# Division by the sums behind the product with the values, in a hybrid layer of pooling and sliding-window attention

## Chip, cores and metric

The kernel runs on one core of a Trainium2 chip. Its time is the device time of one launch in microseconds (us); smaller is better. A core has TensorE (PE: products of matrices, and the loads of their weights, PEld), VectorE (DVE), ScalarE (ACT), GpSimd (POOL) and SyncE (SP, which issues most transfers). They run side by side, each through its own list of instructions in order, and wait for one another by semaphores. SBUF is the working memory of 128 partitions, PSUM holds TensorE's results in eight banks.

## The reference

One layer, 1024 tokens, width 1024, all in float32. What is computed, cut to what matters:

```python
h = rmsnorm(x, norm_pre)
pool_u, pool_gate, q, k, v, attn_gate = split(h @ w_in)          # widths 512, 512, 512, 128, 128, 512
# pooling: trailing means over 2, 4, 8 and 16 tokens (one window for each 128 channels), minus the token
pooled = means(pool_u) - pool_u
pool_out = (pooled @ w_grp per group) * scale * silu(pool_gate)
# attention: 8 heads of 64, 2 heads of keys and values, blocks of 128 queries against 256 keys
scores = q @ k.T * 64 ** -0.5 - slope * distance                 # window of 128, causal
probs  = softmax(concat([scores, sink], -1))[..., :-1]           # one sink logit for each head
attn_out = (probs @ v) * silu(attn_gate)
y = concat([pool_out, attn_out]) @ w_out
x = x + rmsnorm(y, norm_post)
```

So a row of probabilities is exp(score - m) over the sum of these and exp(sink - m), with m the largest of the row and the sink.

## The kernel before

Every product in float32 is made of three float16 products: an operand is scaled by a power of two and split into a high and a low half (`split`: ScalarE writes the high half, VectorE the low one). The power of two comes from a bound: ScalarE sums absolute values (`bound_w`), TensorE spreads the 128 sums over the partitions (`spread`), VectorE reduces them (`widest`) and makes the scale (`pow2_of`, together `scale_w`).

Ahead of the loop x is normed and transposed into `hT`, and the weights of K, V and Q are prepared; `v_tile` makes V in eight pieces. Then a written-out order runs over slots s = 5 to 33. A slot is one projection of 128 channels by 512 tokens (`proj`, 24 matmuls): the rest of K and Q for the second half of the tokens (5 to 9), the pool's gates `pg` (10 to 17), the pool's inputs `u` (18 to 25) and the attention's gates `ag` (26 to 33). `land_slot` takes each result out of PSUM. All instructions stand in the order in which the code names them; nothing reorders them later.

Block n of attention has slots 5 + 2n and 6 + 2n. In the even one of a pair `score_mm` makes the scores (four banks), `score_land` scales them on VectorE, adds the bias and reduces the maximum, and ScalarE makes eight exponentials with their sums. `soft` (odd slot) adds the sink's exponential, takes the reciprocals (8 for each query) and GpSimd multiplies the 1024 values. `turn` (next even slot) splits them into `ph`, which a transposing transfer turns into `full`; `mask` (odd) cuts it on GpSimd by two selections into the block's own keys and the previous ones; `pv_mm` (two slots after that) makes the product with V, which ScalarE takes into `cat`, ahead of the gate.

For a weight of slot s0, `bound_w` stands in slot s0 - 3, `spread_w` at the end of s0 - 2, `scale_w` at the start of s0 - 1. Weights come by `load_next` in the order of `loads_in_order` through four buffers, each load once a buffer is given up. The pool's windows (`pool_windows`, VectorE) follow one slot behind their input, `pool_mm` one more. After the last slot TensorE runs 16 products of the output projection (`out_mm`) back to back.

PSUM: three banks for projections and V (`ps_acc`), four (`ps_b`, taken by `bank`) for scores, transposes, spread bounds and the pool, one for the product with the values. The names that the rows use: `st` the scores, `negm` the negated maximum, `whl` a split weight, `wraw` and `woraw` raw weights, `amall` a reduced bound, `ws` its scale, `wom` the output weight's bound, `acc` a projection, `tp` a transpose, `pv` a piece of V.

Of the kernel before, what the change touches and what calls it, by code (L numbers as in the profile page):

```python
# [35 lines left out]
def trunk(ctx: ExitStack, tc, x, w_in, pool_w, pool_scale, attn_sinks, w_out, norm_pre, norm_post, out):  # L36
# [21 lines left out]
    def work(name):  # L58
        return t4.tile([P, S], F32, tag="t4", name=name)
# [201 lines left out]
    def v_tile(tt):  # L261
        w = whl[V]
        pv = ps_acc.tile([P, 512], F32, tag="acc", name="pv")[:, :P]
# [15 lines left out]
    nsinks = const.tile([P, 8], F32, name="nsinks")  # L279
    pscale = const.tile([P, 4], F32, name="pscale")  # L280
    pw = const.tile([P, 4, P], F32, name="pw")
    post = const.tile([P, D], F32, name="post")
# [16 lines left out]
    def constants():  # L299
        nc.gpsimd.tensor_scalar(nsinks, sinks, -1.0, 0.0, op0=ALU.mult, op1=ALU.add)  # L300
# [29 lines left out]
    att_sc, att_s, att_p, att_f = {}, {}, {}, {}  # L330
# [18 lines left out]

    def score_land(n):  # L350
        st = work("st").rearrange("p (h s) -> p h s", s=P)
        for pr in range(2):
            for kv, sc in enumerate(att_sc.pop((n, pr))):
                hs = slice(4 * kv + 2 * pr, 4 * kv + 2 * pr + 2)
                if n:
                    nc.vector.copy_predicated(sc[:, :, 0, :], own_key.bitcast(U16), sc[:, :, 1, :])  # L356
                nc.vector.scalar_tensor_tensor(  # L357
                    st[:, hs, :], sc[:, :, 0 if n else 1, :], qu[:, 2 * pr : 2 * pr + 1],
# [13 lines left out]
        nc.scalar.activation(es, es, AF.Exp)  # L372
        att_s[n] = (st, sums, es)

    def soft(n):
        st, sums, es = att_s[n]
        nc.vector.tensor_tensor(sums, sums, es, op=ALU.add)
        r = small.tile([P, 8], F32, tag="r", name="r")
        nc.vector.reciprocal(r, sums)
        nc.gpsimd.tensor_tensor(st, st, r.unsqueeze(2).broadcast_to([P, 8, P]), op=ALU.mult)  # L380


    def turn(n):
        st = att_s.pop(n)[0]
        ph = att.tile([P, 2, 8, P], F16, tag="ph", name="ph")
        split(st, 4096.0, ph[:, 0], ph[:, 1])
# [3 lines left out]
        )  # L390
        att_f[n] = full

# [16 lines left out]

    def pv_mm(n):  # L410
# [4 lines left out]
        for tt, t in parts:  # L415
# [60 lines left out]
    def land_slot(ch, half, acc):  # L476
# [6 lines left out]
        elif kind == "pg":  # L483
            nc.scalar.activation(cat[:, c, hs], acc, AF.Silu, scale=wu[ch])
# [28 lines left out]
    def open_late():  # L513
        att.release()
        lp = ctx.enter_context(tc.tile_pool(name="late", bufs=1, reuse_waits="tile"))
        late["wo"] = lp.tile([P, 2, KT, D], F16, name="wo")

# [47 lines left out]
    def out_last(n):  # L565
        o, xr = work(f"o{n}"), residue.pop(n)
        for nh in range(2):
            hs = half_of(nh)
            acc = out_mm(n, nh)
            nc.vector.tensor_tensor(o[:, hs], acc, post[:, hs], op=ALU.mult)  # L570
# [9 lines left out]
    def out_store(n, accs):  # L580
# [4 lines left out]
        for nh, acc in enumerate(accs):  # L585
            hs = half_of(nh)
            nc.vector.scalar_tensor_tensor(  # L587
                o[:, hs], acc, f, post[:, hs], op0=ALU.mult, op1=ALU.mult
# [5 lines left out]
    with tc.manual_schedule(engines={ENG.PE, ENG.Activation, ENG.DVE, ENG.Pool, ENG.SP}):  # L594
# [87 lines left out]
        def loads_in_order():  # L682
            for i in range(3):
                yield "w", PGS[i]
            yield "b", 0
            yield "w", PGS[3]
            for k in range(1, 6):
                yield "b", k
            yield "w", US[0]
            yield "b", 6  # L690
            yield "w", US[1]
            yield "b", 7
            for ch in US[2:] + AGS:
                yield "w", ch
# [15 lines left out]
        wo_bound = split_done = 0  # L710
        last = len(slots)
        for s in range(5, last):
# [4 lines left out]
            for key in list(spreads):  # L717
                if key[0] == "c":
                    scale_cat(key[1])
                elif key[0] == "wo":  # L720
                    pow2_of(widest(spreads.pop(key)), wop, wos, 14)
                else:
                    scale_w(key)
# [105 lines left out]
```

## Time and profile before

| | us |
|---|---|
| median of 3 runs | 388.57 |
| lowest and highest | 387.72, 389.57 |
| the profiled execution | 391.86 |
| its span, first to last instruction | 390.1 |
| TensorE busy in the span | 334.8 (86%) |
| VectorE busy | 205.1 (53%) |
| ScalarE busy | 178.9 (46%) |
| GpSimd busy | 75.6 (19%) |
| TensorE's granted clock, share of 2.4 GHz | 0.949 |

Busy time is a sum over stages that differ, so it doesn't tell what bounds; a stage's own waits do. Matmuls overlap and their ends are modelled, so a busy TensorE isn't one at its peak. The times of the table's first two lines come from runs without the profiler.

### The profile page before, as it was taken

The numbers are of one execution on the slowest core, as the hardware profiler recorded it, in microseconds if no ns is written. First come the engines' busy times: TensorE is split into PE (matmuls) and PEld (weight loads), VectorE is DVE, ScalarE is ACT, GpSimd is POOL, SyncE is SP. The second block draws the span as 40 slices with busy tenths as digits, with TensorE's granted clock in tenths as the row PEclk, the third lists the DMA queues.
The fourth block names the chain that finished last, engine by engine and source line by source line (L and its number), as shares of the span: only waits on it lengthen the run. The fifth ranks groups of instructions, "written<-read, shape, count | busy, mean of one in ns | idle before, by whom it ended". The sixth has DMA issues, their size and how long they took to land.

```text
span 390.1 us, 4820 instructions
## 1 busy us (share of the span) xinstructions
PE 334.8 (86%) x1783; PEld 161.2 (41%) x1783; DVE 205.1 (53%) x435; ACT 178.9 (46%) x374; POOL 75.6 (19%) x74
## 2 busy tenths in 40 slices
PE   3487799999796969908995999997999999999993
PEld 1355557444342424403441344442444444444441
DVE  2776563326665736438388854677467144441122
ACT  5656552054639484884834322355546323321110
POOL 1101023010141414160504140000000033333330
PEclk9999699999896999966999699999999999999998
DMA  7963303002243745535251240045810022225111
GB/s 275 247 177 83 109 2 109 0 2 54 60 103 108 161 103 115 86 78 126 50 108 41 55 109 0 4 154 146 244 48 0 0 89 86 84 95 172 70 55 54
DMA packets 52089, 35.71 MB, mean 92 GB/s; under 512 B 35041, under 2 KB 45793, under 8 KB 52066
## 3 DMA queue, kind: packets, MB, share of 16 engines
q1 hardware_dynamic: 52064, 35.40, 34.1%
q8 instruction: 14, 0.23, 0.2%
q14 instruction: 9, 0.07, 0.1%
q10 hardware_dynamic: 2, 0.00, 0.0%
HBM read 27.01 MB, written 4.19 MB: 80 GB/s over the span
## 4 chain that ended last, share of the span: by engine, by line
PE 37%; DVE 27%; ACT 17%; issue 11%; POOL 4%; DMA 2%; SPq 0%; DVEq 0%; POOLq 0%; ACTq 0%
PE acc L259 20%; PE y L259 11%; ACT st L368 4%; ACT whl L93 4%; DVE st L357 3%; POOL o L590 3%; DVE win L452 2%; DVE sc L356 2%; PE pv L259 2%; DVE whl L94 2%; DVE negm L363 2%; DVE negm L362 2%; DVE ph L94 2%; ACT whl L90 2%; DVE wo L94 2%
## 5 line engine op out<-in xcount | busy, mean ns | idle before, releaser
L259 PE MATMUL acc<-hT,whl 128*128 128x512 f16 x816 | 190.4, 391 | 8.0 <-ACT whl L93 5.2
L259 PEld LDWEIGHTS <-whl 128*128 128x128 f16 x816 | 79.6, 100 | 114.1 <-issue 16.7
L259 PE MATMUL y<-wo,chl 128*128 128x512 f16 x384 | 83.5, 379 | 0.0
L259 PEld LDWEIGHTS <-chl 128*128 128x128 f16 x384 | 37.6, 98 | 44.5
L368 ACT ACTIVATE st<-st,negm 128x128 f32<-128x128 f32 x64 | 24.8, 388 | 42.2 <-DVE negm L363 42.2
L94 DVE SCALAR_TENSOR_TENSOR whl<-wraw,ws,whl 128x1024 f16<-128x1024 f32 x18 | 23.1, 1294 | 28.9 <-ACT whl L93 27.6
L559 ACT ACTIVATE junk<-y 128x512 bf16<-128x512 f32 x16 | 9.6, 597 | 57.1 <-PE y L259 57.1
L93 ACT ACTIVATE whl<-wraw,ws 128x1024 f16<-128x1024 f32 x18 | 20.4, 1144 | 29.7 <-DVE ws L76 29.7
L561 DVE SCALAR_TENSOR_TENSOR eps_of<-yss,eps_of 128x1 f32<-128x1 f32 x16 | 4.6, 288 | 48.3 <-ACT junk L559 48.1
L400 POOL TENSOR_SCALAR_AFFINE_SELECT own<-full 128x2048 f16<-128x2048 f16 x7 | 14.0, 2006 | 66.5 <-DMA full<-ph 52.1
L380 POOL TENSOR_TENSOR st<-st,r 128x1024 f32<-128x1024 f32 x8 | 15.2, 1896 | 56.8 <-ACT whl L90 19.5
L582 POOL TENSOR_TENSOR yf<-eps_of,mhalf 128x1 f32<-128x1 f32 x7 | 3.9, 551 | 108.1 <-DVE eps_of L561 108.1
L342 PE MATMUL sc<-kT,qT 64*128 64x256 f16 (+1 forms) x192 | 15.4, 297 | 9.3 <-DVE amall L86 8.8
L243 PE MATMUL tp<-ident,h 128*128 128x128 f32 x64 | 12.9, 368 | 11.8 <-DVE h L234 10.8
L590 POOL TENSOR_TENSOR o<-o,xr 128x512 f32<-128x512 f32 x14 | 17.4, 1268 | 17.7 <-DVE o L587 13.9
L90 ACT ACTIVATE whl<-wraw 128x1024 bf16<-128x1024 f32 x18 | 18.8, 1047 | 0.0
L94 DVE SCALAR_TENSOR_TENSOR qT<-acc,qT 128x512 f16<-128x512 f32 x8 | 5.5, 691 | 22.8 <-ACT qT L93 22.8
L243 PEld LDWEIGHTS tp<-ident,h 128*128 128x128 f32 x64 | 10.6, 193 | 15.3 <-DVE h L234 6.8
L259 PE MATMUL pv<-whl,hT 128*128 128x128 f16 x192 | 12.6, 230 | 4.2 <-DVE vst L94 4.2
L342 PEld LDWEIGHTS <-qT 64*128 64x128 f16 x192 | 9.7, 103 | 15.1 <-issue 12.3
L357 DVE SCALAR_TENSOR_TENSOR st<-sc,qu,bias 128x256 f32<-128x256 f32 x32 | 15.2, 483 | 1.1
L94 DVE SCALAR_TENSOR_TENSOR chl<-cat,cs,chl 128x1024 f16<-128x1024 f32 x8 | 10.3, 1284 | 10.2 <-ACT chl L93 10.2
(106 smaller groups left out, 371.2 us busy)
## 6 DMA issues: line engine op xcount, KB each, us to landing
wraw<-in_w_in_dram SPq DMA_DIRECT2D x10, 512.0 KB, 4.4
x<-in_x_dram SPq DMA_DIRECT2D x8, 512.0 KB, 5.6
wraw<-in_w_in_dram SPq DMA_DIRECT2D x16, 256.0 KB, 4.0
woraw<-in_w_out_dram SPq DMA_DIRECT2D x8, 512.0 KB, 4.2
woraw<-in_w_out_dram SPq DMA_DIRECT2D x16, 256.0 KB, 4.8
xr<-in_x_dram SPq DMA_DIRECT2D x8, 512.0 KB, 3.6
out_dram<-o SPq DMA_DIRECT2D x16, 256.0 KB, 2.0
post<-in_norm_post_dram SPq DMA_DIRECT2D x1, 512.0 KB, 4.7
```

Source lines behind the costliest of these rows:

```text
L90: nc.scalar.activation(junk, src, AF.Abs, accum_out=m)
L93: nc.scalar.activation(hi, src, AF.Copy, scale=s)
L94: eng.scalar_tensor_tensor(lo, src, s, hi, op0=ALU.mult, op1=ALU.subtract)
L243: nc.tensor.transpose(flips[tt][b][:, block_of(i)], h[:, block_of(4 * b + i)], ident)
L259: nc.tensor.matmul(acc, a, b, start=i == 0, stop=i == len(pairs) - 1)
L342: nc.tensor.matmul(banks[kv][:, ci, k0:, :], qT[rows, a, 2 * pr + ci, block_of(n)], kT[rows, b, (n - 1 + k0) * P : (n + 1) * P], start=i = ...
L357: nc.vector.scalar_tensor_tensor(st[:, hs, :], sc[:, :, 0 if n else 1, :], qu[:, 2 * pr : 2 * pr + 1], (bias if n else bias0)[:, hs, :], o ...
L368: nc.scalar.activation(st[:, h, :], st[:, h, :], AF.Exp, bias=negm[:, h : h + 1], accum_out=sums[:, h : h + 1],)
L380: nc.gpsimd.tensor_tensor(st, st, r.unsqueeze(2).broadcast_to([P, 8, P]), op=ALU.mult)
L400: nc.gpsimd.affine_select(o, f, pattern=[[0, 16], [1, P]], compare_op=ALU.is_ge, fill=0.0, base=0, channel_multiplier=-1,)
L559: nc.scalar.activation(junk, acc, AF.Square, accum_out=q)
L590: nc.gpsimd.tensor_tensor(o[:, hs], o[:, hs], xr[:, hs], op=ALU.add)
```

## The change

The values of a block are no longer divided by their sums ahead of the split. `turn` stands in the odd slot of the block, directly behind the exponentials, `mask` in the next even one, `pv_mm` in the next odd one. VectorE takes the reciprocals with each sum repeated 64 times (512 elements for each query); in the next even slot `divide` turns them by four transposes on TensorE, ScalarE puts them into `cat` with V's scale, and VectorE multiplies the product with V into that. The sink is a 129th score column, copied in by VectorE, so the maximum and the sums hold it. `Silu` of the pool's gates is taken out of `land_slot` and done in slots 20 to 23, in place, on 1024 elements. Spread bounds, and the transposed reciprocals, have a bank of their own (`ps_sp`); `ps_acc` has two banks instead of three, and V's pieces take theirs from the four of `ps_b`. A weight is spread and scaled at the start of s0 - 2. The weights of the gates and inputs are loaded ahead of the output weight's first pass, whose bounds move from slots 8 to 18 to slots 19 to 22; the split of the output weight starts once its bound is there. `post` lives in a later pool and is loaded when that opens, at slot 22.

The diff, cut to its core:

```diff
-    ps_acc = ctx.enter_context(tc.tile_pool(name="ps_acc", bufs=3, space=PSUM))
+    ps_acc = ctx.enter_context(tc.tile_pool(name="ps_acc", bufs=2, space=PSUM))
+    ps_sp = ctx.enter_context(tc.tile_pool(name="ps_sp", bufs=1, space=PSUM))
...
     def spread(m):
-        t = bank("spread", P)
+        t = ps_sp.tile([P, 512], F32, tag="sp", name="spread")[:, :P]
...
     def v_tile(tt):
-        pv = ps_acc.tile([P, 512], F32, tag="acc", name="pv")[:, :P]
+        pv = bank("pv", P)
...
     def score_land(n):
-        st = work("st").rearrange("p (h s) -> p h s", s=P)
+        st = t4.tile([P, S + 8], F32, tag="t4", name="st").rearrange("p (h s) -> p h s", h=8)
+        nc.vector.tensor_copy(st[:, :, P], sinks)
...
         nc.vector.tensor_reduce(negm, st, axis=AX.X, op=ALU.max, negate=True)
-        nc.vector.tensor_tensor(negm, negm, nsinks, op=ALU.min)
-        es = small.tile([P, 8], F32, tag="es", name="es")
-        nc.vector.tensor_tensor(es, sinks, negm, op=ALU.add)
...
-        nc.scalar.activation(es, es, AF.Exp)
-        att_s[n] = (st, sums, es)
-
-    def soft(n):
-        st, sums, es = att_s[n]
-        nc.vector.tensor_tensor(sums, sums, es, op=ALU.add)
-        r = small.tile([P, 8], F32, tag="r", name="r")
-        nc.vector.reciprocal(r, sums)
-        nc.gpsimd.tensor_tensor(st, st, r.unsqueeze(2).broadcast_to([P, 8, P]), op=ALU.mult)
+        att_s[n] = (st, sums)
...
     def turn(n):
-        st = att_s.pop(n)[0]
+        st, sums = att_s.pop(n)
...
+        r = t2.tile([P, 512], F32, tag="t2", name="r")
+        nc.vector.reciprocal(
+            r.rearrange("p (c kv d) -> p c kv d", c=4, kv=2),
+            sums.rearrange("p (kv c) -> p c kv", kv=2).unsqueeze(3).broadcast_to([P, 4, 2, HD]),
+        )
...
+    def divide(n):
+        r = att_r.pop(n)
+        rb = ps_sp.tile([P, 512], F32, tag="sp", name="rb")
+        for c in range(4):
+            nc.tensor.transpose(rb[:, block_of(c)], r[:, block_of(c)], ident)
+        nc.scalar.activation(
+            cat[:, 4:8, block_of(n)], rb.rearrange("p (c t) -> p c t", t=P), AF.Copy, scale=vo
+        )
...
-        nc.scalar.activation(
-            cat[:, 4:8, block_of(n)], pv.rearrange("p (c t) -> p c t", t=P), AF.Copy, scale=vo
-        )
+        dst = cat[:, 4:8, block_of(n)]
+        nc.vector.tensor_tensor(dst, pv.rearrange("p (c t) -> p c t", t=P), dst, op=ALU.mult)
...
         elif kind == "pg":
-            nc.scalar.activation(cat[:, c, hs], acc, AF.Silu, scale=wu[ch])
+            nc.scalar.activation(cat[:, c, hs], acc, AF.Copy, scale=wu[ch])
...
         def loads_in_order():
-            for i in range(3):
-                yield "w", PGS[i]
-            yield "b", 0
-            yield "w", PGS[3]
-            for k in range(1, 6):
+            for ch in PGS + US:
+                yield "w", ch
+            for k in range(6):
                 yield "b", k
...
+                elif first_slot[key] == s + 2:
+                    spread_w((key,))
+                    scale_w((key,))
                     freed += 1
             if not odd:
                 if 1 <= n <= NB:
-                    turn(n - 1)
+                    mask(n - 1)
                 if n < NB:
                     score_mm(n)
             else:
+                if n < NB:
+                    turn(n)
                 if 1 <= n <= NB:
-                    mask(n - 1)
-                if 2 <= n <= NB + 1:
-                    pv_mm(n - 2)
-                if n < NB:
-                    soft(n)
+                    pv_mm(n - 1)
             acc = proj(ch, half)
...
+            if 20 <= s < 24:
+                gate = cat[:, 23 - s, :]
+                nc.scalar.activation(gate, gate, AF.Silu)
...
-            if not odd and n < NB:
-                score_land(n)
+            if not odd:
+                if n < NB:
+                    score_land(n)
+                if 1 <= n <= NB:
+                    divide(n - 1)
```

VectorE's order in one pair of slots with two weights, from the maximum of block 2. Before (`sums` and `r` are the softmax's, the three rows from `amall` make a weight's scale):

```order
L362 TENSOR_REDUCE negm<-st 128x8
L363 TENSOR_TENSOR negm<-negm,nsinks 128x8
L365 TENSOR_TENSOR es<-sinks,negm 128x8
L94 SCALAR_TENSOR_TENSOR qT<-acc,qT 128x512
L86 TENSOR_REDUCE amall<-spread 128x1
L72 TENSOR_SCALAR wp<-amall 128x1
L75 TENSOR_SCALAR wp<-wp 128x1
L76 RECIPROCAL ws<-wp 128x1
L94 SCALAR_TENSOR_TENSOR whl<-wraw,ws,whl 128x1024
L216 TENSOR_TENSOR wu<-wp,gsc 128x1
L377 TENSOR_TENSOR sums<-sums,es 128x8
L379 RECIPROCAL r<-sums 128x8
```

and after the change, from the same maximum:

```order
L362 TENSOR_REDUCE negm<-st 128x8
L95 SCALAR_TENSOR_TENSOR qT<-acc,qT 128x512
L87 TENSOR_REDUCE amall<-spread 128x1
L73 TENSOR_SCALAR wp<-amall 128x1
L76 TENSOR_SCALAR wp<-wp 128x1
L77 RECIPROCAL ws<-wp 128x1
L95 SCALAR_TENSOR_TENSOR whl<-wraw,ws,whl 128x1024
L217 TENSOR_TENSOR wu<-wp,gsc 128x1
L95 SCALAR_TENSOR_TENSOR ph<-st,ph 128x1024
L381 RECIPROCAL r<-sums 128x512
L430 TENSOR_TENSOR cat<-pvo,cat 128x4x128
L87 TENSOR_REDUCE amall<-spread 128x1
```

The two instructions on the sinks are gone; the split `ph` of the same block has come up behind the first weight, and a reciprocal of 512 elements and the product with the values stand between it and the second weight.

GpSimd's order over the same blocks (`st` scaled by `r`, then the two selections). Before:

```order
L380 TENSOR_TENSOR st_871<-st_871,r_894 128x1024
L380 TENSOR_TENSOR st_985<-st_985,r_1012 128x1024
L400 AFFINE_SELECT own_1164<-full_1065 128x2048
L404 AFFINE_SELECT full_1065<-full_1065 128x2048
L380 TENSOR_TENSOR st_1123<-st_1123,r_1176 128x1024
```

and after:

```order
L395 AFFINE_SELECT own_1082<-full_1025 128x2048
L399 AFFINE_SELECT full_1025<-full_1025 128x2048
L395 AFFINE_SELECT own_1250<-full_1188 128x2048
L399 AFFINE_SELECT full_1188<-full_1188 128x2048
L395 AFFINE_SELECT own_1383<-full_1339 128x2048
```

GpSimd's scaling has gone; the selections alone are left.

## Rows read from the trace of the kernel before

**Rows 1.** Busy time by stretch: us, then engines (instructions), PEclk, DMA share, GB/s.
```profile
0.00:74.24 74.24, 55.78 (x384) 36.31 (x385) 38.86 (x79) 36.38 (x65) 10.42 (x30) 0.95 0.47 132
74.24:89.18 14.94, 14.42 (x104) 7.12 (x104) 6.91 (x17) 6.94 (x23) 1.90 (x1) 1.00 0.01 1
89.18:200.09 110.91, 89.76 (x505) 40.70 (x503) 61.92 (x137) 71.78 (x172) 31.48 (x16) 0.89 0.43 95
200.09:231.71 31.62, 26.28 (x112) 10.44 (x111) 24.07 (x47) 9.36 (x26) 9.94 (x5) 0.89 0.39 84
231.71:300.70 68.99, 65.05 (x295) 28.66 (x294) 44.41 (x87) 33.18 (x45) 0.00 (x0) 1.00 0.29 84
300.70:390.10 89.40, 83.48 (x389) 37.98 (x387) 28.97 (x73) 21.27 (x46) 21.85 (x22) 0.99 0.22 77
```

**Rows 2.** TensorE's waits: for whom, us in total, times, longest.
```profile
PE spread L81 <- DVE wom L748: 9.0, 1, 9.0
PE sc L342 <- DVE amall L86: 8.8, 5, 3.4
```

**Rows 3.** Timeline of VectorE, blocks 1, 6, 7: start, us, operation, [idle before].
```profile
89.18 0.42 DVE L356 COPY_PREDICATED sc<-own_key,sc 128x256 f32<-128x256 uint16 x1
...
180.36 0.42 DVE L356 COPY_PREDICATED sc<-own_key,sc 128x256 f32<-128x256 uint16 x1
...
185.16 0.17 DVE L363 TENSOR_TENSOR negm<-negm,nsinks 128x8 f32<-128x8 f32 x1
...
198.96 1.22 DVE L94 SCALAR_TENSOR_TENSOR ph<-st,ph 128x1024 f16<-128x1024 f32 x1
200.09 0.42 DVE L356 COPY_PREDICATED sc<-own_key,sc 128x256 f32<-128x256 uint16 x1
```

**Rows 4.** VectorE's groups by shape: busy us, mean ns, idle before.
```profile
L491 DVE TENSOR_TENSOR cat<-cat,gt 128x512 f32<-128x512 f32 x8 | 5.5, 687 | 3.6 <-ACT gt L489 3.6
...
L76 DVE RECIPROCAL ws<-wp 128x1 f32<-128x1 f32 x16 | 2.6, 163 | 0.6
...
L379 DVE RECIPROCAL r<-sums 128x8 f32<-128x8 f32 x8 | 1.6, 203 | 0.3
...
L305 DVE RECIPROCAL invc<-cnt 128x16 f32<-128x16 f32 x1 | 0.2, 241 | 0.0
```

**Rows 5.** Timeline of ScalarE and VectorE from block 2's exponentials.
```profile
112.20 0.40 ACT L368 ACTIVATE st<-st,negm 128x128 f32<-128x128 f32 x1 [6.98 <-DVE negm L363]
...
115.29 0.19 ACT L372 ACTIVATE es<-es 128x8 f32<-128x8 f32 x1
...
116.61 0.28 DVE L86 TENSOR_REDUCE amall<-spread 128x1 f32<-128x128 f32 x1
...
117.55 1.15 ACT L93 ACTIVATE whl<-wraw,ws 128x1024 f16<-128x1024 f32 x1 [1.59 <-DVE ws L76]
118.61 0.67 ACT L424 ACTIVATE cat<-pvo,vo 128x512 f32<-128x512 f32 x1
119.17 1.04 ACT L90 ACTIVATE whl<-wraw 128x1024 bf16<-128x1024 f32 x1
```

**Rows 6.** Timeline: VectorE beside GpSimd, and SyncE's transposing transfer.
```profile
105.78 1.88 SPq L388 DMA_TRANSPOSE full<-ph  x1
...
110.14 2.01 POOL L400 TENSOR_SCALAR_AFFINE_SELECT own<-full 128x2048 f16<-128x2048 f16 x1 [9.11 <-DMA full<-ph]
110.47 1.70 DVE L363 TENSOR_TENSOR negm<-negm,nsinks 128x8 f32<-128x8 f32 x1
...
193.71 1.90 POOL L380 TENSOR_TENSOR st<-st,r 128x1024 f32<-128x1024 f32 x1 [1.61 <-DVE ug L441]
...
194.63 1.01 DVE L442 COPY tails<-ug 128x16 f32<-128x16 f32 x1 [1.04 <-ACT ug L437]
```

**Rows 7.** Timeline of TensorE ahead of the loop: V's last piece, eight transposes.
```profile
41.39 2.72 PE L259 MATMUL pv<-whl,hT 128*128 128x128 f16 x24 [4.20 <-DVE vst L94]
...
57.55 1.04 PE L243 MATMUL tp<-ident,h 128*128 128x128 f32 x8
```

More of the change, by code (lines that the diff above doesn't have):

```diff
@@ L299, in constants @@
     def constants():
-        nc.gpsimd.tensor_scalar(nsinks, sinks, -1.0, 0.0, op0=ALU.mult, op1=ALU.add)
         cnt = const.tile([P, 16], F32, name="cnt")
@@ L516, in open_late @@
         late["wo"] = lp.tile([P, 2, KT, D], F16, name="wo")
+        late["post"] = lp.tile([P, D], F32, name="post")
+        nc.sync.dma_start(late["post"], norm_post[0:1, :].partition_broadcast(P))
     def split_wo(k):
@@ L569, in out_last @@
             acc = out_mm(n, nh)
-            nc.vector.tensor_tensor(o[:, hs], acc, post[:, hs], op=ALU.mult)
+            nc.vector.tensor_tensor(o[:, hs], acc, late["post"][:, hs], op=ALU.mult)
         f = col("yf")
@@ L587, in out_store @@
             nc.vector.scalar_tensor_tensor(
-                o[:, hs], acc, f, post[:, hs], op0=ALU.mult, op1=ALU.mult
+                o[:, hs], acc, f, late["post"][:, hs], op0=ALU.mult, op1=ALU.mult
             )
@@ L710, in trunk @@
         wo_bound = split_done = 0
+        wo_ready = False
         last = len(slots)
@@ L715, in trunk @@
             freed = 0
[L717 to L723, printed above, removed]
+            for key in list(bounds):
+                if key[0] in ("wo", "c"):
+                    spreads[key] = spread(bounds.pop(key))
+                    if key[0] == "c":
+                        scale_cat(key[1])
+                    else:
+                        pow2_of(widest(spreads.pop(key)), wop, wos, 14)
+                        wo_ready = True
+                elif first_slot[key] == s + 2:
+                    spread_w((key,))
+                    scale_w((key,))
                     freed += 1
@@ L741, in trunk @@
                     bound_w(c2)
-            if s >= 8 and ("b", wo_bound) in wo_raw:
-                bound_wo(wo_bound)
-                freed += 1
-                wo_bound += 1
-                if wo_bound == KT:
-                    m = bounds["wo", 0] = col("wom")
-                    nc.vector.tensor_reduce(m, wom, axis=AX.X, op=ALU.max)
+            if 20 <= s < 24:
+                gate = cat[:, 23 - s, :]
+                nc.scalar.activation(gate, gate, AF.Silu)
+            if s >= 19:
+                for _ in range(2):
+                    if ("b", wo_bound) in wo_raw:
+                        bound_wo(wo_bound)
+                        freed += 1
+                        wo_bound += 1
+                        if wo_bound == KT:
+                            m = bounds["wo", 0] = col("wom")
+                            nc.vector.tensor_reduce(m, wom, axis=AX.X, op=ALU.max)
             if s >= 30:
                 bound_cat(s - 30)
-            if s >= 26:
+            if wo_ready:
                 for _ in range(2 if s < 28 else 1):
@@ L763, in trunk @@
             land_slot(ch, half, acc)
-            for key in list(bounds):
-                if key[0] in ("wo", "c"):
-                    spreads[key] = spread(bounds.pop(key))
-                elif first_slot[key] == s + 2:
-                    spread_w((key,))
-            if s == 5 + 2 * (NB + 1) + 1:
+            if s == 5 + 2 * NB + 1:
                 open_late()
-                nc.sync.dma_start(post, norm_post[0:1, :].partition_broadcast(P))
             for _ in range(freed):
@@ L775, in trunk @@
                 load_res(s - last + 2)
-        for key in list(spreads):
+        for key in list(bounds):
+            spreads[key] = spread(bounds.pop(key))
             scale_cat(key[1])
```

17 lines of the change are left out of this document (8 added, 9 removed).

## The prediction

> **What bounds the kernel now.** I read the busy times by stretch first [rows 1]. From 74.24 to 89.18 us and behind 231.71 TensorE works 93 to 97% of the time, with 0.99 to 1.00 of its 2.4 GHz granted; up to 74.24, while the inputs come in, 75%. From 89.18 to 231.71 it works 81 and 83%, and 0.89 is granted, so part of the time it runs at 1.2 GHz. There is something to win in that attention stretch, and a little ahead of it. Next come TensorE's waits [rows 2]: its 8.8 us for `amall` are the scores' waits for a bank that a spread bound holds, the 9.0 us are one wait for the bounds of the output weight. But why are VectorE and ScalarE late, when in that stretch they work only 61.92 and 71.78 of 110.91 us [rows 1]? The timeline of VectorE answers it [rows 3]: they take turns. The scores of a block are landed and reduced (180.36 to 185.16, 4.8 us), ScalarE takes the eight exponentials (112.20 to 115.29 in another block, 3.1 us [rows 5]), then come a landing, weight splits, the split of `ph`, and only then the next block's scores (200.09). I call that from one landing's start to the next one's a round. From block 1 (89.18) to block 7 (200.09) there are six rounds in 110.9 us, 18.5 each. TensorE needs less: 89.76 us of work in six rounds [rows 1], 15.0 each, or 13.3 at the full clock (x 0.89). So the round of VectorE and ScalarE sets the pace, and the change is judged by what it does to that round.
>
> **Part by part.** (1) *The round's new member.* Before, a round holds a reciprocal of 8 elements (0.20 us) and GpSimd's scaling (1.90 us in one block [rows 6]) ahead of `ph`. Now `ph` comes straight from the exponentials, but VectorE's reciprocal has 512 elements, the sums already repeated 64 times, and stands in VectorE's order before the next block's landing. Its form isn't in the trace. From above and below: 1, 8 and 16 elements took 163, 203 and 241 ns [rows 4], so an element costs 5.2 ns over the whole distance (4.8 to 5.7 over its halves), and 512 cost 0.163 + 511 x 5.2 ns = 2.8 us (2.6 to 3.1). Were it as quick as another VectorE instruction of 512 elements, it would be 0.69 us (`cat<-cat,gt` [rows 4]). I take 2.8, as the nearest rows are reciprocals and grow by five times what the other forms do.
> The Trainium skill, VectorE: DVE Perf Modes, section Walkthrough: the 8-slice pipeline in each mode, says that a reciprocal is an iterated division with a repeat count of 8. An estimate from that page at 0.96 GHz is 8.3 ns an element and 4.4 us; the rows up to 16 elements say 5.2 ns, and by the page the sum below would be some 11 us higher.
> (2) *Rounds without weights* (blocks 3 to 5): landing 4.8, exponentials 3.1, two ScalarE evictions (the spread reciprocals and a projection) 0.6 each by their distance in [rows 5], ScalarE's `ph` 1.0, VectorE's `ph` 1.2, reciprocal 2.8, the product with the values 0.7 and the sinks' copy 0.2: 15.0, with hops 15.15. TensorE's work for a block is then 13.3 + 0.5 for four more transposes (half of 1.04 [rows 7]), 13.8: the round still bounds.
> (3) *Rounds with two weights* (1 to 3 and 5 to 7): a bound's reduction to a weight's split is 0.94 (116.61 to 117.55 [rows 5]), ScalarE's split 1.1, VectorE's 1.2 (like `ph` [rows 3]). The second weight adds 0.94 + 1.1 + 1.2 behind the product, the first adds about 1.4, since ScalarE's `ph` hides behind VectorE's split: 19.85. Where a query is also landed (0.7 and the chain behind it, 1.0) it is 21.6, with two queries 22.05. The weights' steps now come one slot earlier, so both of a pair fall in one round. Without any new wait the six rounds are 22.05 + 21.6 + 2 x 15.15 + 2 x 19.85 = 113.65, 2.7 above today's 110.9.
> (4) *A lock between VectorE and GpSimd.* At 110.47 a VectorE instruction of 8 elements took 1.70 us [rows 6] where it takes 0.17 alone (185.16 [rows 3]), and ended with GpSimd's selection (110.14 + 2.01); at 194.63 a copy of 16 elements took 1.01 and ended with GpSimd's product (193.71 + 1.90) [rows 6]. GpSimd's two selections of 2.0 us follow `ph`'s transposed copy by 4.4 us (105.78 to 110.14), so they run 4.5 to 8.5 us behind VectorE's `ph`. The second weight's split on VectorE stands at 5.7 to 6.2 there: it waits for the first selection, holds the second back, and the sinks' copy behind it waits for that one's end. The landing starts at 9.9 instead of 7.3 to 7.7: 2.4 more in each of the four rounds with weights, 9.6 in all. The landing's own instructions read PSUM and ran beside GpSimd undisturbed.
> The Trainium skill, SBUF — State Buffer, section SBUF: two separate sides, gives the rule: GpSimd and VectorE share a pair of ports, held for a whole instruction, and a VectorE copy at double rate, or one with two SBUF inputs, is shut out. That agrees with the 1.70 and 1.01; by it the splits and the sinks' copy count, and the sum is the forecast's; without it the sum is 13.6 lower.
> (5) *Block 7 to the last stretch* (before 200.09 to 231.71, 31.6). Now: landing 4.8, four window sums and a difference 4.0, `ph` and its wait 2.6, reciprocal 2.8, two products 1.4, the next windows 3.3, of which GpSimd's selections shut out some 4.0 more, then TensorE's pool product, the last attention product, a projection and a pool product, 8.6: 31.4. So -0.2 (-4.2 without the lock).
> (6) *Start of the loop.* The fourth product of V no longer waits for a bank of the accumulators (4.20 us [rows 7]), but the transposes behind it now wait for the same landing. What is saved is that product, 2.72 [rows 7], or half of it, 1.4, if it took that long at the lower clock: -1.5, from -1.2 to -3.7. Block 1's landing loses its waits on the sinks: -0.6.
> (7) *Last loop stretch* (231.71 to 300.70, 68.99 for 65.05 of work [rows 1]): the last attention product, 1.4, is now ahead of it, and of the 3.9 us in which TensorE rests there, mostly for late weight splits, I let 1.7 go, since VectorE stays full and makes the pool products late instead: -3.1 (-1.4 to -5.3). The output weight's bounds move behind the attention; their transfers have three slots to land, so I put that at nothing, and at the 9.0 of [rows 2] if not.
> (8) At nothing: 32 transposes of 0.13 us on TensorE [rows 7], some 4 us, hidden in its slack of 1.4 us a round, and 4 more if a round came down to TensorE's work; the Silu of the gates and its one table load, beside VectorE's windows; the sinks as a 129th column, 8 x 1 element.
> **Sum:** -1.5 - 0.6 + 2.7 + 9.6 - 0.2 - 3.1 = +6.9. The profiled execution took 391.86 us (span 390.1, and 1.8 around it), the runs' median is 388.57, 0.85% less; I add the change to the median: 388.57 + 6.9 = **395.5**.
>
> **The rivals.**
> A. *The long reciprocal is cheap* (0.69 us): the other side. It is VectorE's instruction behind each `ph`; seven stand on the path. Rounds without weights fall to TensorE's 13.8; those with two lose 2.1, and the sinks' copy meets the end of the first selection only (1.2): six rounds 107.3, and the part behind block 7 loses 2.1. Sum -1.5 - 0.6 - 3.6 - 2.3 - 3.1 = -11.1: 377.5. It decides below about 1.8 us a piece (6.9 / 7 less than 2.8). Against it: the three reciprocals' rows.
> B. *The sinks' copy isn't shut out*, only the splits are. Then a round with weights loses 0.5, not 2.4: -0.7, 387.9. For it: only one copy shows the wait; against: that one ended with GpSimd's instruction to 0.05 us.
> C. *No lock here at all*, since the selections come later or the transfer is slower: -6.7, 382.
> D. *A reciprocal costs more*: the steeper slope gives 3.1 us, 7 x 0.3 more, 397.5. By the page named above it would be 406.
>
> **How the numbers follow.** Forecast (rounds as in 2 to 5) 0.56; A 0.12; B 0.18; C 0.06; D 0.08. The forecast's own range is 391 to 400, as my sums of rounds may be off by 0.7 us each. The range 381 to 403 leaves out A and the page's end of D. What a measurement of this kernel can tell from no change is about 0.5%, 1.9 us. Slower by more: the forecast's 0.53 and D 0.08, 0.61; within: 0.03 and two thirds of B, 0.15; faster: A, C and a third of B, 0.24.
>
> **What would show it.** The row of the reciprocal with 512 elements: near 2.8 us, or A or D. The first landing of block 7: 123 us behind that of block 1 by the forecast, 114 without the lock, 107 by A. The sinks' copy: 0.15 in rounds without weights, 1.5 to 2.0 in the four with them. TensorE's waits: none for `amall` by the scores, long ones for the bounds ahead of the last spread of each pair (5 us and more), and none of 9.0 for the output weight; if that one is there, (7) is wrong. If TensorE works over 90% between blocks 1 and 7, the round isn't what bounds, and the argument falls.

## The result: 403.0 us, slower by 3.7%

The changed kernel takes 403.0 us (median of 4 runs, 402.25 to 404.28). Against the kernel before the ratio is 1.0373, with a 95% interval of 1.0327 to 1.0419; one further run of the kernel before, of 496.57 us where the other three lie within 2, isn't counted. The forecast was slower, 395.5 us, a ratio of 1.018: the direction was right, the size half of what came, and the time lies at the upper end of the range. The profiled execution took 404.28 us, with a span of 402.6.

First the busy time by stretch, cut at the places that answer to those of [rows 1]: block 1's landing, block 7's landing, the start of slot 23, the start of the output projection. Columns as there: us, then PE, PEld, DVE, ACT, POOL busy (instructions), PEclk, DMA share, GB/s.

```profile
0.00:86.19 86.19, 69.90 (x484) 41.82 (x485) 48.33 (x95) 43.21 (x87) 10.42 (x29) 0.92 0.45 117
86.19:212.41 126.22, 101.78 (x549) 46.19 (x547) 82.86 (x133) 53.29 (x145) 24.95 (x12) 0.84 0.25 57
212.41:246.09 33.68, 25.77 (x116) 11.04 (x115) 24.61 (x42) 19.33 (x42) 4.71 (x2) 0.90 0.70 163
246.09:313.13 67.04, 63.05 (x285) 28.49 (x282) 45.51 (x92) 32.22 (x42) 0.00 (x0) 1.00 0.33 91
313.13:402.60 89.47, 83.48 (x390) 38.04 (x387) 28.73 (x70) 21.60 (x46) 21.86 (x22) 0.99 0.22 77
```

Set beside [rows 1] (there, the first two stretches together are the first here) and beside the terms of the prediction:

| stretch, us | before | forecast | after |
|---|---|---|---|
| start to block 1's landing | 89.18 | -2.1 | 86.19 (-3.0) |
| six rounds, block 1 to block 7 | 110.91 | +12.3 | 126.22 (+15.3) |
| block 7 to slot 23 | 31.62 | -0.2 | 33.68 (+2.1) |
| slots 23 to 33 | 68.99 | -3.1 | 67.04 (-1.9) |
| output projection | 89.40 | 0 | 89.47 (+0.1) |
| sum | 390.10 | +6.9 | 402.60 (+12.5) |

So the profiles differ by 12.5 us, 5.6 more than forecast. The other 1.9 of the miss of 7.5 is the base: the profiled execution before lay 3.3 us above its median, the one after only 1.3 (404.28 and 403.0), and the forecast added its sum to the median.

What TensorE waits for (for whom, us in total, times, longest) answers to [rows 2]:

```profile
PE spread L82 <- ACT cat L411: 21.5, 4, 7.8
...
PE spread L82 <- ACT whl L91: 3.9, 3, 1.9
```

The scores' wait for `amall` and the wait of 9.0 us for the output weight are gone. Four waits of a spread stand in their place. A spread bound and the transposed reciprocals share the one bank of `ps_sp`, and ScalarE empties it into `cat` only behind the next block's exponentials.

One round shows how it goes, block 5's landing to block 6's. VectorE first (start, us, operation, [idle before]), from the end of the round ahead of it:

```profile
159.17 1.23 DVE L95 SCALAR_TENSOR_TENSOR ph<-st,ph 128x1024 f16<-128x1024 f32 x1 [5.35 <-ACT ph L94]
160.31 3.35 DVE L381 RECIPROCAL r<-sums 128x512 f32<-128x512 f32 x1
163.58 0.63 DVE L430 TENSOR_TENSOR cat<-pvo,cat 128x512 f32<-128x512 f32 x1
164.12 0.16 DVE L351 COPY st<-sinks 128x8 f32<-128x8 f32 x1
164.19 0.42 DVE L356 COPY_PREDICATED sc<-own_key,sc 128x256 f32<-128x256 uint16 x1
...
173.32 0.29 DVE L87 TENSOR_REDUCE amall<-spread 128x1 f32<-128x128 f32 x1 [4.36 <-PE spread L82]
...
182.81 0.29 DVE L87 TENSOR_REDUCE amall<-spread 128x1 f32<-128x128 f32 x1 [1.05 <-PE spread L82]
...
184.95 2.74 DVE L95 SCALAR_TENSOR_TENSOR whl<-wraw,ws,whl 128x1024 f16<-128x1024 f32 x1 [1.28 <-ACT whl L94]
```

TensorE in the same round:

```profile
168.66 0.60 PE L410 MATMUL rb<-ident,r 128*128 128x128 f32 x4
172.81 0.47 PE L82 MATMUL spread<-ident,as 128*128 128x128 f32 x1 [3.55 <-ACT cat L411]
...
175.91 6.75 PE L260 MATMUL acc<-hT,whl 128*128 128x512 f16 x24
182.50 0.27 PE L82 MATMUL spread<-ident,as 128*128 128x128 f32 x1
182.70 1.48 PE L340 MATMUL sc<-kT,qT 64*128 64x256 f16 x24
184.12 5.35 PE L260 MATMUL acc<-hT,whl 128*128 128x512 f16 x24
```

Each weight of the pair is late. The first one's bound is spread at 172.81, behind ScalarE's copy. The second one's spread stands in TensorE's order behind a projection that the first wait has pushed back, and that projection takes 6.75 us where the same 24 matmuls take 5.35 at 184.12: from 172.81 to 175.91, right behind the wait, 0.50 of the clock is granted (1.2 of 2.4 GHz), over this projection 0.78, at 184.12 all of it. So `amall` waits at 173.32 (4.36) and at 182.81 (1.05). The second split then falls on GpSimd's selections (182.53 to 184.54 and 184.60 to 186.61) and takes 2.74 us where it takes 1.28 alone.

### The profile page after: what moved, and what is told of

It is laid out like the page before. It is cut to its first block, busy times and chain, and to the rows that moved or that the text cites. A ratio compares the mean times of both kernels' runs of the same rounds, so it can differ in the third digit from the quotient of the medians.

```text
span 402.6 us, 4859 instructions
## 1 busy us (share of the span) xinstructions
PE 344.0 (85%) x1815; PEld 165.6 (41%) x1815; DVE 230.0 (57%) x427; ACT 169.7 (42%) x360; POOL 61.9 (15%) x65
## 4 chain that ended last, share of the span: by engine, by line
PE 41%; DVE 30%; ACT 13%; issue 9%; POOL 3%; DMA 2%; DVEq 0%; SPq 0%; POOLq 0%; ACTq 0%
PE acc L260 23%; PE y L260 10%; ACT st L365 5%; DVE st L357 4%; DVE win L456 4%; DVE r L381 3%; PE pvo L423 3%; DVE whl L95 3%; POOL o L596 2%; DVE negm L362 2%; DVE sc L356 2%; ACT whl L94 2%; PE pv L260 1%; DMA wraw<-in_w_in_dram 1%; PE mixed L473 1%
## 5 line engine op out<-in xcount | busy, mean ns | idle before, releaser
L260 PEld LDWEIGHTS <-whl 128*128 128x128 f16 x816 | 81.3, 101 | 106.8 <-issue 23.8
L365 ACT ACTIVATE st<-st,negm 128x129 f32<-128x129 f32 x64 | 24.8, 389 | 49.3 <-DVE negm L362 49.3
L95 DVE SCALAR_TENSOR_TENSOR whl<-wraw,ws,whl 128x1024 f16<-128x1024 f32 x18 | 26.2, 1463 | 20.4 <-ACT whl L94 19.1
L82 PE MATMUL spread<-ident,as 128*128 128x128 f32 x24 | 7.8, 325 | 25.4 <-ACT cat L411 21.5
L381 DVE RECIPROCAL r<-sums 128x512 f32<-128x512 f32 x8 | 26.8, 3346 | 0.0
L244 PE MATMUL tp<-ident,h 128*128 128x128 f32 x64 | 12.0, 350 | 13.4 <-DVE h L235 10.8
L95 DVE SCALAR_TENSOR_TENSOR ph<-st,ph 128x1024 f16<-128x1024 f32 x8 | 9.8, 1222 | 11.7 <-ACT ph L94 11.7
L473 PE MATMUL mixed<-res,pw 128*128 128x512 f32 x16 | 9.4, 672 | 8.0 <-DVE ug L445 6.8
L82 PEld LDWEIGHTS spread<-ident,as 128*128 128x128 f32 x24 | 3.6, 152 | 30.5 <-ACT cat L411 22.4
```

Of the source, the lines that this page charges most:

```text
L95: eng.scalar_tensor_tensor(lo, src, s, hi, op0=ALU.mult, op1=ALU.subtract)
L244: nc.tensor.transpose(flips[tt][b][:, block_of(i)], h[:, block_of(4 * b + i)], ident)
L260: nc.tensor.matmul(acc, a, b, start=i == 0, stop=i == len(pairs) - 1)
L365: nc.scalar.activation(st[:, h, :], st[:, h, :], AF.Exp, bias=negm[:, h : h + 1], accum_out=sums[:, h : h + 1],)
L381: nc.vector.reciprocal(r.rearrange("p (c kv d) -> p c kv d", c=4, kv=2), sums.rearrange("p (kv c) -> p c kv", kv=2).unsqueeze(3).broadcast ...
L473: nc.tensor.matmul(acc, pw[:, c, :], pool_out.pop((c, half)), start=True, stop=True)
```

## The experiments

All rounds in one table, each from the first predicated copy of a block's landing to the next block's, in us (the forecast's rows are from parts 2 to 4 of the prediction). The fifth and sixth rounds hold the weights of the inputs, the first and second those of the gates.

| kernel | 1-2 | 2-3 | 3-4 | 4-5 | 5-6 | 6-7 | sum |
|---|---|---|---|---|---|---|---|
| before | 16.49 | 21.16 | 18.94 | 16.22 | 18.37 | 19.73 | 110.9 |
| forecast | 24.45 | 24.00 | 15.15 | 15.15 | 22.25 | 22.25 | 123.3 |
| forecast without the lock | 22.05 | 21.60 | 15.15 | 15.15 | 19.85 | 19.85 | 113.7 |
| after | 24.00 | 23.73 | 15.13 | 15.14 | 23.56 | 24.66 | 126.2 |
| e3, no selections | 22.12 | 21.50 | 15.14 | 15.13 | 22.24 | 22.09 | 118.2 |
| e2, bank | 23.90 | 23.74 | 15.13 | 15.14 | 22.24 | 22.26 | 122.4 |
| e10, bank, no selections | 22.11 | 21.51 | 15.14 | 15.13 | 19.90 | 20.06 | 113.9 |
| e1, short reciprocal | 21.55 | 23.73 | 12.50 | 15.97 | 23.14 | 23.92 | 120.8 |
| e12, short and bank | 21.29 | 18.88 | 12.79 | 14.12 | 17.27 | 19.24 | 103.6 |
| e9, and early bounds | 21.23 | 18.81 | 12.80 | 14.07 | 17.21 | 17.36 | 101.5 |
| e11, and small ones on ScalarE | 19.21 | 18.62 | 12.97 | 13.94 | 17.08 | 17.15 | 99.0 |
| e7, Silu back | 24.04 | 23.76 | 16.55 | 16.54 | 23.68 | 26.10 | 130.7 |
| e5, before, long reciprocal | 17.94 | 22.30 | 22.15 | 17.89 | 20.07 | 21.50 | 121.9 |

Times, with the ratio to the kernel before on the same chip:

| kernel | median us | ratio, 95% interval |
|---|---|---|
| e1, short reciprocal | 393.25 | 1.0151, 1.0082 to 1.0220 |
| e2, bank | 398.78 | 1.0270, 1.0242 to 1.0299 |
| e3, no selections | 391.89 | 1.0090, 1.0064 to 1.0115 |
| e12, short and bank | 375.81 | 0.9668, 0.9635 to 0.9702 |
| e5, before, long reciprocal | 404.94 | 1.0404, 1.0358 to 1.0451 |
| e6, V's pieces back | 407.33 | 1.0473, 1.0435 to 1.0511 |
| e7, Silu back | 408.45 | 1.0501, 1.0460 to 1.0542 |
| e9, and early bounds | 374.04 | 0.9606, 0.9564 to 0.9648 |
| e10, bank, no selections | 388.82 | 0.9980, 0.9949 to 1.0010 |
| e11, and small ones on ScalarE | 371.69 | 0.9537, 0.9477 to 0.9597 |

### e1, e2, e12: the long reciprocal, the bank, and both

```diff
-        nc.vector.reciprocal(r (512 wide), sums repeated 64 times)
+        nc.vector.reciprocal(rs, sums)
+        nc.vector.tensor_copy(r (512 wide), rs repeated 64 times)
```
```diff
-        rb = ps_sp.tile([P, 512], F32, tag="sp", name="rb")
+        rb = bank("rb")
```

The first is e1, the second e2, both together e12.

> The changed kernel, but VectorE takes 8 reciprocals for each query (0.20 us before the change) and a copy repeats them 64 times, where one reciprocal of 512 elements took 3.35 us. Theory R, the long reciprocal stands on the path: 2.5 us less for each block; rounds with weights 24.0, 23.7, 23.6, 24.7 each lose 2.5, the two without fall from 15.1 to TensorE's work of 13.8, and the part behind block 7 loses 2.5: -15, 388 us. Theory S, the one bank for spreads and transposed reciprocals sets the rounds with weights (the spread waits for ScalarE's copy behind the exponentials, whatever VectorE does): only the two rounds without weights and a part of the rest move, -3 to -6, 397 to 400 us.

> The changed kernel, but the transposed reciprocals take one of the four banks of ps_b, so no spread waits for ScalarE's copy of them (21.5 us of TensorE's waits in four places). Theory S, that bank sets the four rounds with weights: -8 us or more, 395 us or less. Theory R: VectorE's row stays as full; only where nothing else lies ahead of the reduced bound does it come earlier (1.0 us in each of the two rounds of the inputs' weights, once again 1.0 where it waits for the spread): -3 to -4 us, 399 to 400 us, with the 21.5 gone from TensorE's waits all the same.

> Both edits: 8 reciprocals and a copy that repeats them, and the transposed reciprocals in a bank of ps_b. Theory R: the gain of the short reciprocal (-15) and that of the bank (-3 to -4) add up: 384 to 385 us, below the kernel before. Rival: with the short reciprocal the rounds fall on TensorE's work and the chain of the weights' bounds, and the bank gives no more than 1 us on top: 387 to 388 us.

e1 came out at 393.25 us, 9.8 less than the changed kernel (8.6 by the ratios; its four runs spread from 391.75 to 397.48), between the two theories. e2 at 398.78, 4.2 less, 0.2 beyond theory R's range. e12 at 375.81, 27.2 less: 13 more than the two gains together, which no theory expected.

The table tells why. e1 takes the full 2.5 from the first round and the third, but nothing from the second, and the fourth grows. Its instructions on VectorE (groups by shape: busy us, mean ns, idle before):

```profile
L383 DVE COPY r<-rs 128x512 f32<-128x512 f32 x8 | 3.4, 427 | 0.3
L382 DVE RECIPROCAL rs<-sums 128x8 f32<-128x8 f32 x8 | 1.6, 196 | 0.0
```

So the reciprocals cost 0.6 us instead of 3.35. But in the second round of e1 TensorE still stands still for the bank (timeline of TensorE):

```profile
114.12 0.47 PE L82 MATMUL spread<-ident,as 128*128 128x128 f32 x1 [7.92 <-ACT cat L413]
...
117.22 6.21 PE L260 MATMUL acc<-hT,whl 128*128 128x512 f16 x24
123.27 0.27 PE L82 MATMUL spread<-ident,as 128*128 128x128 f32 x1
```

and VectorE, done earlier, waits for that second spread and then meets a selection (timeline of VectorE, e1):

```profile
123.58 0.29 DVE L87 TENSOR_REDUCE amall<-spread 128x1 f32<-128x128 f32 x1 [2.60 <-PE spread L82]
...
127.28 1.95 DVE L217 TENSOR_TENSOR wu<-wp,gsc 128x1 f32<-128x1 f32 x1
```

From the end of the exponentials to the next landing there are two chains side by side. One is VectorE's row: split, `ph`, the long reciprocal, product. The other runs through TensorE: ScalarE's copy, first spread, product with the values, a slow projection, second spread, second split. With the long reciprocal the two are about equally long in the second round; in the fifth and sixth TensorE's is the longer, by 0.9 and 1.7 us (e1 against e2). Either edit alone shortens one of them and leaves the other to end the round; both together take 4.9, 6.3 and 5.4 us from the second, fifth and sixth rounds. Not all of that is the chains'. In e1 and e2 GpSimd's selections hold a product for 1.95 us in the second and the fifth round; in e12 they begin as the next landing does (125.72, 169.99) and hold nothing. That wait costs 2.2 and 2.3 us in these two rounds (e2 against e10 below), so up to that much of e12's gain there is the selections'; no run parts the two. In e12 TensorE no longer waits for the bank at all, and the busy row of its fifth round (columns as in the first fence) shows TensorE without a gap, at the full clock:

```profile
152.70:169.97 17.27, 17.27 (x115) 8.49 (x112) 10.99 (x26) 11.21 (x28) 4.01 (x2) 1.00 0.28 48
```

### e3, e10: GpSimd's selections, alone and with the bank

```diff
-        nc.gpsimd.affine_select(o, f, ...)
-        nc.gpsimd.affine_select(f, f, ...)
-        att_p[n] = [(n, own), (n - 1, full)]
+        att_p[n] = [(n, full), (n - 1, full)]
```

> The changed kernel without GpSimd's two selections: the masked halves of the probabilities are left out as a step, and both halves of the product read the transposed copy as it is. Theory L, the lock between GpSimd and VectorE as the prediction has it, 2.4 us in each of four rounds and 4 us behind block 7: -13.6, 389 us. By the stretched rows of the trace (splits of 2.96 and 2.74 for 1.28 us, a product of 1.95 for 0.15, windows of 4.80 for 1.4) it is 4.9 in the rounds and up to 3.4 behind block 7: -8, 395 us. If the stretched instructions would have waited for something else anyhow: -3 or less, 400 us or more.

> The changed kernel without GpSimd's two selections (that step is left out) and with the transposed reciprocals in a bank of ps_b; the long reciprocal stays. Taking away either alone left 22.1 to 22.3 us for each of the two rounds with the inputs' weights, of 23.6 and 24.7. Theory H, the bank's wait and the lock hide one another: with neither, these rounds take the 19.9 of the prediction's sum, six rounds 113.7 in all, 5 us less than without the selections alone: 386 to 388 us. Rival, something else holds these rounds at 22.2: 391 us as without the selections alone.

e3 took 391.89 us, 11.1 less: between the forecast's 13.6 and the 8 read from stretched rows. Its six rounds fall by 8.0, where the forecast had put 9.6 for the lock, and the first four are those of the forecast without the lock to 0.1 us. The last two are not: 22.24 and 22.09 for 19.85. That is the point on which e10 decides. With the bank freed as well they come to 19.90 and 20.06, and all six rounds to 113.9 for a forecast of 113.7, as theory H had it; the time, 388.82 us, lies 0.8 above its range and 2.2 below the rival's. So it is the bank that holds these two rounds at 22.2 without the selections. That the two waits hide one another holds for the fifth round alone: there either edit gives 1.3 us and both 3.7. In the sixth they nearly add up, 2.4 and 2.6 alone and 4.6 together.

Which rows were shut out? The split above (2.74 for 1.28 us), a split of 2.96, a product of 1.95 for 0.15, and in the sixth round this copy (VectorE, then GpSimd, of the changed kernel):

```profile
207.17 1.85 DVE L446 COPY tails<-ug 128x16 f32<-128x16 f32 x1 [1.77 <-ACT ug L441]
```
```profile
206.99 2.01 POOL L395 TENSOR_SCALAR_AFFINE_SELECT own<-full 128x2048 f16<-128x2048 f16 x1 [20.38 <-DMA full<-ph]
209.07 2.01 POOL L399 TENSOR_SCALAR_AFFINE_SELECT full<-full 128x2048 f16<-128x2048 f16 x1
```

The copy ends with the first selection (207.17 + 1.85, 206.99 + 2.01). It isn't whatever VectorE comes to. Shut out were copies within SBUF and instructions with two inputs there, as small as 16 elements or one. The landing's predicated copies and scalings, which read PSUM, keep their 0.42 and 0.48 us beside selections (149.91 and 150.36), and what has one input in SBUF keeps its time too: the maximum its 1.23 us (152.59), a scale's two steps and its reciprocal their 0.15 and 0.16 (183.13 to 183.67). The Trainium skill, SBUF — State Buffer, section SBUF: two separate sides, says that GpSimd and VectorE share a pair of ports, which one instruction holds to its end, against VectorE's copies at double rate and its instructions with two SBUF inputs. These runs agree, with 8.0 us in six rounds as the price here.

### e5: the long reciprocal in the kernel before

```diff
-        nc.vector.reciprocal(r, sums)
+        nc.vector.reciprocal(rl (512 wide), sums repeated 64 times)
+        r = rl[:, :, 0]
```

> The kernel before with one part of the change alone: VectorE takes its reciprocals with each sum repeated 64 times (3.35 us for 0.20), GpSimd's product reads one of each 64. Theory R, in the kernel before the row of VectorE sets each round: 3.15 us in each of six rounds and behind block 7, 19 to 22 us more, 408 to 411 us. Theory P, a second chain runs beside VectorE's row (TensorE's projections, with their weights, up to the scores) and hides part of what is added: 8 to 13 us more, 397 to 402 us.

404.94 us, 16 more; the profiles differ by 14.0. Neither theory's range holds it. The rounds grow by 1.1 to 3.2 us, 10.9 in all, not by 6 x 3.15. In the fifth round (+1.70) one can see where the rest went. VectorE (kernel before, then e5):

```profile
166.79 0.17 DVE L363 TENSOR_TENSOR negm<-negm,nsinks 128x8 f32<-128x8 f32 x1
...
174.96 0.16 DVE L748 TENSOR_REDUCE wom<-wom 128x1 f32<-128x8 f32 x1 [3.30 <-ACT junk L90]
```
```profile
175.37 1.88 DVE L363 TENSOR_TENSOR negm<-negm,nsinks 128x8 f32<-128x8 f32 x1
...
180.81 3.35 DVE L379 RECIPROCAL r<-sums 128x512 f32<-128x512 f32 x1
...
185.25 0.16 DVE L749 TENSOR_REDUCE wom<-wom 128x1 f32<-128x8 f32 x1 [1.09 <-ACT junk L90]
```

The row had a gap of 3.30 us behind the reciprocal, and 2.21 of the new 3.15 went into it. The other 0.94 took the place of a hold: `sums`, ahead of the reciprocal, took 1.11 us beside a selection before (170.31) and takes 0.17 in e5. So in this round the reciprocal itself costs nothing, and the 1.70 is the lock's: `negm` now meets a selection (175.23 + 2.00) and takes 1.88 us for 0.17, and ScalarE's exponentials, with the sum `junk` that ends the gap, come 1.70 later behind the landing's start. So a round isn't the sum of VectorE's and ScalarE's work in every kernel: gaps behind the changed instruction count against it. In the changed kernel no such gap is left there (164.12 follows 163.58 above), which is why the third and fourth rounds, summed up link by link, came out at the forecast.

### e6, e7: V's pieces, and Silu, as before

```diff
-        pv = bank("pv", P)
+        pv = ps_acc.tile([P, 512], F32, tag="acc", name="pv")[:, :P]
```
```diff
-            nc.scalar.activation(cat[:, c, hs], acc, AF.Copy, scale=wu[ch])
+            nc.scalar.activation(cat[:, c, hs], acc, AF.Silu, scale=wu[ch])
...
-            if 20 <= s < 24:
-                gate = cat[:, 23 - s, :]
-                nc.scalar.activation(gate, gate, AF.Silu)
```

> The changed kernel with V's pieces back in the banks of the accumulators, of which there are two now. The start of block 1's landing moved from 89.18 to 86.12 us with the change. If V's own banks gave that (the wait of 4.20 us of the kernel before comes back, and a bank is missing besides): 1.5 to 4 us more, 404.5 to 407 us. If the landing without waits on the sinks gave it: no difference, 403 us.

> The changed kernel with Silu of the pool's gates back where each gate is taken out of PSUM, between the exponentials of two blocks, so that ScalarE changes between the tables of Exp and Silu (1.28 us each in the trace, ten loads in the kernel before, one in the changed one). The prediction put moving them at nothing: 403 us, at most 1 us off. Rival: ScalarE stands on the path where it loads the table of Exp ahead of the exponentials: 1.28 to 2.56 us in each of the blocks 3 to 6, 5 to 10 us more, 408 to 413 us.

e6: 407.33 us, 0.3 above the first range, by the ratios 3.9 more than the changed kernel; block 1's landing starts at 90.61 us, 4.4 later. V's banks bring that, and the wait is back (TensorE's waits, e6):

```profile
PE pv L260 <- DVE vst L95: 4.5, 1, 4.5
```

e7: 408.45 us, by the ratios 5.0 more: the rival. The third and fourth rounds grow by 1.4 each and the sixth by 1.4, and in the third this table load stands between ScalarE's last work for a block and its split into `ph` (timeline of ScalarE, e7):

```profile
140.28 0.67 ACT L411 ACTIVATE cat<-rb,vo 128x512 f32<-128x512 f32 x1
...
140.95 1.28 ACT L488 ACT_TABLE_LOAD   x1
142.25 0.69 ACT L488 ACTIVATE cat<-acc,wu 128x512 f32<-128x512 f32 x1
142.83 1.05 ACT L94 ACTIVATE ph<-st 128x1024 f16<-128x1024 f32 x1
```

There the load back to Exp's table falls into a wait of ScalarE (144.47, 163.05). In the sixth round it is the other way round: the load of Exp's table starts only once the maximum is there, and the exponentials wait for it, while Silu's falls mostly into a wait:

```profile
193.99 1.28 ACT L365 ACT_TABLE_LOAD   x1 [7.53 <-DVE negm L362]
```

In the second and fifth rounds no load is on the path (0.03 and 0.12 us more). So of two loads a block, one at most is.

### e9, e11: two steps beyond e12

```diff
             for c2 in order:
-                if first_slot[c2] == s + 3:
+                if not odd and 0 <= first_slot[c2] - s - 3 < 2 and c2 not in whl and c2 in raws:
+                    bound_w(c2)
+                elif odd and first_slot[c2] == s + 3 and c2 not in whl:
                     bound_w(c2)
```
```diff
-        nc.vector.tensor_tensor(u, p, gsc, op=ALU.mult)
+        nc.scalar.activation(u, p, AF.Copy, scale=gsc)
...
-        nc.vector.tensor_copy(st[:, :, P], sinks)
+        nc.scalar.activation(st[:, :, P], sinks, AF.Copy)
```

> The kernel with the short reciprocal and the own bank for the transposed ones (375.8 us), in which TensorE still waits 13.1 us for bounds that ScalarE sums behind the exponentials and a split; here the bound of a pair's second weight is summed in the even slot, ahead of the exponentials. Theory C (what holds TensorE there is ScalarE's queue): the waits fall to some 3 us, and 4 to 8 us go, 368 to 372 us. Rival, VectorE's row carries these rounds anyhow: 374 to 377 us.

> The kernel with short reciprocal, own bank and early bounds (374.0 us), and two small operations on ScalarE instead of VectorE: the weights' product of one element for each partition, which took 1.95 us beside a selection in one round, and the sinks' copy. Theory L, what the lock costs there is these 1.95 us: 372 us. Rival, VectorE's next operation is shut out instead, or ScalarE's row grows as much: 374 us or more.

e9: 374.04 us. TensorE's waits for ScalarE's sums fell from 13.1 to 1.9 us, as theory C had it, and the time by 1.8 only, as its rival had it: those waits were mostly not on the path. TensorE's waits for a landing ahead of the transposed reciprocals rose at the same time, from 2.5 to 7.6 us. Of the 2.1 us that the six rounds gained, 1.9 came in the sixth, where in e12 the sinks' copy had met a selection (187.24 + 2.03) and in e9 takes 0.17 (VectorE, e12):

```profile
187.31 1.99 DVE L351 COPY st<-sinks 128x8 f32<-128x8 f32 x1
```

e11: 371.69, as theory L had it; the first round fell from 21.23 to 19.21, by what the product had waited. This one is 4.6% faster than the kernel before (ratio 0.9537, 0.9477 to 0.9597).

## Why the prediction was right and wrong

**What bounds.** Right for four of the six rounds. VectorE's and ScalarE's turns set them, and without lock and bank (e10) all six follow from the links of parts 2 and 3 to 0.2 us in 113.7. In the last two the chain through the bank set the pace beside them, see (3). TensorE works 101.78 of 126.22 us in the changed kernel, 81%, not over 90.

**(1) The reciprocal.** It took 3.35 us where the straight line through the short ones gave 2.8; an element costs 6.2 ns ((3346 - 163) / 511) instead of 5.2. The row, of all eight:

```profile
L381 DVE RECIPROCAL r<-sums 128x512 f32<-128x512 f32 x8 | 26.8, 3346 | 0.0
```

Rival A is out, D half came true, and that it cost the sum nothing is luck: two errors cancel. In the rounds without weights the other links were as much shorter, since VectorE's instructions follow one another closer than their lengths say: from the start of `ph` (159.17) to the landing (164.19) it is 5.02 us for a forecast of 1.2 + 2.8 + 0.7 + 0.2 = 4.9.
The Trainium skill, VectorE: DVE Perf Modes, section Walkthrough: the 8-slice pipeline in each mode, with its repeat count of 8, had given an estimate of 4.4 us; the row lies a third of the way from the line to that, and decides.

**(2) Rounds without weights.** 15.13 and 15.14 for 15.15.

**(3) Rounds with two weights: the step that failed.** The first two came at 22.1 and 21.5 without the lock, for 22.05 and 21.6. The last two were put at 19.85 and took 22.2 without the lock, 4.6 us more in the two. The sum was made "without any new wait": it took a reduced bound as being at hand when the exponentials end. The prediction's own tells named long waits for the bounds ahead of each pair's last spread and gave them no price; what came were 21.5 us ahead of the first spread, for the bank that it shares with the transposed reciprocals. Where a query is landed there first, VectorE's queue covers the wait; where not, the bank decides: freed of it, in e10, the two rounds take 19.90 and 20.06.

**(4) The lock.** Its place was right and its size near: 8.0 us for 9.6 (e3), 8.6 with the bank freed (e2 against e10), in the four rounds named. The rows were others. Splits, a product and a small copy ahead of the sinks' copy were shut out; the copy itself comes behind them in these rounds, when the second selection has ended or is within 0.1 us of its end, and it takes 0.16 to 0.17 us in each block. That doesn't bear out rival B: in e12 the sinks' copy did meet a selection, and took 1.99 us. And that the landing runs undisturbed beside GpSimd was no reading of the trace before, where none of its instructions that read PSUM stands beside GpSimd's; the changed kernel is the first to show it.

**(5) Block 7 to slot 23.** 33.68 for 31.4. Without the selections it is 30.70 (e3, 204.42 to 235.12) for the forecast's 27.4, so the lock costs 3.0 there instead of 4.0, and the rest was 3.3 short. Of that, 2.8 is a thing the sum hadn't: TensorE, having waited 3.2 us in e3 for VectorE's windows, does its next pieces at a lower clock, and the four pieces put at 8.6 take 11.4 (223.70 to 235.12). The clock granted is 0.50 up to 228.42, and the pieces take 2.08 us for 1.02, 2.77 for 1.49 and 5.90 for 5.35. In the changed kernel the same follows on its wait of 6.8 us, with 0.50 up to 239.69:

```profile
234.99 2.07 PE L473 MATMUL mixed<-res,pw 128*128 128x512 f32 x2 [6.81 <-DVE ug L445]
...
239.69 5.59 PE L260 MATMUL acc<-hT,whl 128*128 128x512 f16 x24
```

In e1, after a wait of 2.63 us there, the pieces kept to 1.12, 0.84 and 5.35, all at 1.00. The length of the wait isn't what parts the cases: behind one of 3.63 us in the first round 0.50 is granted in the changed kernel (94.81) and 1.00 in e3 (94.83). So the wait alone would not have told these 2.8 us. The remaining 0.5 us is open.

**(6) Start of the loop.** 3.0 us gained for 2.1 forecast. e6 puts V's banks alone at 4.4, with one accumulator bank fewer than before; between kernels with the same start the landing lay anywhere from 83.95 to 86.52 us, so the split between the two parts isn't settled.

**(7) Slots 23 to 33.** 67.04 for 65.9. TensorE's work was near what was put (63.05 us for 63.65), but its rests didn't shrink: 3.9 us of waits, 3.4 of them for late splits, became 3.9 us of waits for late bounds. The output weight's bounds cost nothing, as put.

**(8) At nothing.** Wrong for Silu as it stood there: e7 gives its move 5 us. It did no harm to the sum, since the rounds of part 2 were built from what stands in them after, without table loads. But a reader would have drawn the wrong lesson, and part of the change's gain stayed unnamed.

So the miss of 5.6 us between the profiles is 4.6 in the last two rounds, 2.3 behind block 7, 1.1 in the last slots, less 1.6 for the lock and 0.9 at the start, and 0.1 in the output projection.

## What to carry to other kernels

Behind each instruction that is added or taken away, look for the chain that runs beside it, and for the gap behind it: here two chains of about equal length made either repair worth 4 to 10 us and both together 27, in part because the shorter rounds no longer met GpSimd's selections. A resource that is given to two users in one in-order queue makes the one wait for the other's slowest reader; price that wait wherever nothing else covers it. And repeat a value after the costly operation, not before: 8 reciprocals and a copy took 0.6 us where 512 reciprocals took 3.35, which turned 3.7% slower, with one bank moved, into 3.3% faster.

## What was not expected of the hardware

A reciprocal's cost for each element isn't one number in these rows: 5.7 ns from 1 to 8 elements, 4.8 from 8 to 16 [rows 4], 6.3 from 16 to 512 ((3346 - 241) / 496). An instruction on a single element for each partition can be held for 1.95 us by GpSimd's selection. TensorE came back from a wait of 3.2 us at half its clock (0.50 granted), from one of 2.6 at full clock, and from one of 3.63 at either, by the run.
